# Eleven RMS norms of a two-block transformer: the row of factors by VectorE transposes and a broadcast through DRAM in place of PE products

## The chip, the cores and the metric

One core of a Trainium2 chip. The metric is the device time of one execution in microseconds (us). The engines are PE (matrix products; PEld is its weight load), VectorE (DVE), ScalarE (ACT), GpSimd (POOL) and SyncE (SP); each takes its instructions in the order in which the program has them, and they wait for one another by semaphores.

## What is computed

Two transformer blocks on 512 tokens of width 1024, in fp32. The first mixes by causal softmax attention of eight heads and by four recurrent heads (HGRN), then has a cross attention to a memory and a feed-forward layer; the second mixes by a convolution branch and a state-space branch (SSD, 8 groups of 256 channels) and has a gated feed-forward layer. The change touches two kinds of norm: that of each of the four recurrent heads over its 128 channels, and that of each of the eight groups of the state-space branch over its 256 channels.

```python
def rmsnorm(x, g):
    xf = x.astype(jnp.float32)
    y = xf * lax.rsqrt(jnp.mean(xf * xf, axis=-1, keepdims=True) + EPS)
    return (y * g.astype(jnp.float32)).astype(x.dtype)
...
        rec = hgrn2_chunkwise(gq, gf, gi, lbs[l])
        rec = rmsnorm(rec, hgrn_norm_g[l]) * jax.nn.silu(
            gg.astype(jnp.float32).reshape(b_, s_, HGRN_HEADS, HGRN_VAL_DIM))
...
    y = y * jax.nn.silu(z.astype(f32))
    yg = y.reshape(bsz, seqlen, N_GROUPS, D_INNER // N_GROUPS)
    yg = yg * lax.rsqrt(jnp.mean(yg * yg, axis=-1, keepdims=True) + RMS_EPS)
    y = (yg.reshape(bsz, seqlen, D_INNER) * norm_g.astype(f32)).astype(z.dtype)
    return y @ out_w
```

## The kernel before

Everything lies feature-major: a tile has 128 channels on its partitions and the 512 tokens along its free axis. A gemm (`gemm_tile`) makes one output tile of 128x512 from eight or more weight tiles of 128x128. To keep fp32 precision, weights and activations are split into a high and a low part, and each 128x128 tile is three products (`mm3`, L129 to L131; `wh`, `wl` are the halves of the weights, `xh`, `xl` those of the activations, which after the first block are also called `yh`, `yl` and `uh`, `ul`). A weight block of 128x1024 comes by a DMA on SP's queue, ACT makes its high half (L117), VectorE its low half (L118); each kind has three buffers. L180 and L181 split an activation in the same way.

A norm has four steps. `sq_acc` (L187) squares on ACT and adds up in `sqa` (128x512). `col_sum` (L196) adds over the 128 partitions on PE, four fp32 products with a 128x128 block of `sqa` as the weights and a column of ones (L202), so that the sums of the 512 tokens come out as 128x4. `rsqrt_col` (L206) scales them and adds epsilon on VectorE (`rv`, L208) and raises them to -1/2 on POOL (`rc`, L210). `row_bc` (L213) makes a row for all partitions of these columns, four fp32 products of 128x128 with the identity (L217), into the one PSUM buffer `pc`. A multiplication on VectorE reads it there (L479 in the recurrent heads, L911 in the groups). PE runs an fp32 product in two passes, and the trace has a record for each, so four products stand there as x8.

The first block runs the four recurrent heads (`hgrn_out`) and the attention (`fox`) as a background that is woven into the gemms. Of an attention pair, the scores are L498, the row maxima and sums on VectorE L508 to L516, the transposing products L519, the products with the values L531. Norms 0 and 1 fall near 147 to 170 us, norms 2 and 3 near 261 to 275 us.

The second block's state-space branch takes its 8 groups one after another (`group_a` to `group_b`), some 64 us each, woven into gemms as well. The norm of a group (`group_b`, L899) is done inside the next group's work. There VectorE makes `cb` (L849, the masked C by B product times `tri`), the chunk states `st` (L859 multiplies by the decay, L862 adds a product from PSUM; twice, for chunks 1 and 2 of 3) and the masked decays `mt` (L876); PE then makes the outputs of the group's two halves by products `mt,xd` and `Ct,st` (L885). POOL's queue brings the rows `ab` (L870) and `ep` (L891) from DRAM; ACT makes `mt` of `ab` (L874, L875).

The order of each engine's instructions is fixed when the program is built, by a scheduler that takes whatever is ready by priority; `tc.high_priority(-n)` lets a part come later. `HPRI` is 80, `APRI` 60, `BPRI` 120.

Of the kernel before, what the change touches and what calls it, by code (L numbers as in the profile page):

```python
# [64 lines left out]
def _build(tc, nc, es, a, out):  # L65
# [25 lines left out]
    def ctile(shape, dt, name):  # L91
        return const.tile(shape, dt, tag=name, name=name)

    vec = ctile([P, NVEC], F32, "vec")
    nc.scalar.dma_start(out=vec[:, 0:8], in_=a["vec"][:, 0:8])
    ones = ctile([P, P], F32, "ones")
    V.memset(ones, 1.0)
    mhalf = ctile([P, 4], F32, "mhalf")
    V.memset(mhalf, -0.5)
# [1 line left out]
    A.copy(out=warm, in_=ones[:, 0:4])  # L101
    ident = ctile([P, P], F32, "ident")
    nc.gpsimd.dma_start(out=ident, in_=a["ident"])
    tri = ctile([P, P], F32, "tri")
    nc.gpsimd.dma_start(out=tri, in_=a["tri"])

    def vcol(name, i=0, n=1):
        c, k = VEC[name]
        assert i + n <= k
        return vec[:, c + i:c + i + n]  # L110
# [76 lines left out]
    def sq_acc(accum, k, src, scale=1.0):  # L187
        if k == 0:
            A.activation(out=accum, in_=src, func=AF.Square, scale=scale)
        else:  # L190
            sq = nrm.tile([P, S], F32, tag="sq", name="sq")
            n = accum.shape[-1]
            A.activation(out=sq[:, :n], in_=src, func=AF.Square, scale=scale)
            V.tensor_tensor(out=accum, in0=accum, in1=sq[:, :n], op=ALU.add)
# [18 lines left out]
    def row_bc(col, nt, ms=mA):  # L213

        ps = ms()
        for j in range(nt):
            T.matmul(out=ps[:, j * P:(j + 1) * P], lhsT=col[:, j:j + 1].to_broadcast([P, P]), rhs=ident, start=True,  # L217
                     stop=True)
        return ps[:, :nt * P]

    def norm(srcs, n, nt, gain=None, eps=EPS, pl=None, rtag="R", ms=mA, late=0):

# [78 lines left out]
    with ExitStack() as ea:  # L301
# [163 lines left out]
        def hgrn_out(i, AT):  # L465
            ps = mA()
            for j in range(4):
                T.matmul(out=ps[:, j * P:], lhsT=iT[:, j, i * P:(i + 1) * P],  # L468
                         rhs=AT[:, ab(j, j):ab(j, j) + 4 - j, :].rearrange("p a b -> p (a b)"),
                         start=j == 0, stop=j == 3)  # L470
            o_ = hslot(4 + i)
            mix[4 + i] = o_
            A.copy(out=o_, in_=ps)
            ac = nrm.tile([P, S], F32, tag="sqa", name="sqa")
            sq_acc(ac, 0, o_)
            with tc.high_priority(-HPRI):
                r = rsqrt_col(col_sum(ac, 4, mC), 4, P)
            with tc.high_priority(-2 * HPRI):
                V.scalar_tensor_tensor(out=o_, in0=o_, scalar=vcol("hgrn_norm_g"), in1=row_bc(r, 4, mC), op0=ALU.mult,  # L479
                                       op1=ALU.mult)  # L480

        def fox(pairs):
            PT, nF = {}, {}
# [415 lines left out]
    def group_b(g, ys, zs):  # L899

        ac = nrm.tile([P, S], F32, tag="sqa", name="sqa")
        for e in range(2):
            V.tensor_tensor(out=zs[e], in0=ys[e], in1=zs[e], op=ALU.mult)
            sq_acc(ac, e, zs[e])
        with tc.high_priority(-APRI):
            r = rsqrt_col(col_sum(ac, 4, mC), 4, 256)
        with tc.high_priority(-BPRI):
            Rg = row_bc(r, 4, mC)
            res = []
            for e in range(2):  # L910
                V.scalar_tensor_tensor(out=zs[e], in0=zs[e], scalar=vcol("ssm_norm_g_2", 2 * g + e), in1=Rg, op0=ALU.mult,  # L911
                                       op1=ALU.mult)
                res.append(split_act(zs[e]))
        return res
# [214 lines left out]
def _pack(inp):  # L1129
    import numpy as np  # L1130

    def fm(w):
        K, N = w.shape
        return np.ascontiguousarray(w.reshape(K // P, P, N // P, P).transpose(2, 1, 0, 3))

    def tm(w):
        K, N = w.shape
        return np.ascontiguousarray(w.reshape(K // 256, 2, P, N // S, S).transpose(3, 0, 2, 1, 4))

    g = {}  # L1140
    i = {k: np.asarray(v) for k, v in inp.items()}
    g["xT"] = np.ascontiguousarray(i["x"][0].T)
    g["memT"] = np.ascontiguousarray(i["mem"][0].T)
    w = i["w_in"][0]
    o = [0, 512, 1024, 1536, 1544, 2056, 2568, 3080, 3592]
    p = [w[:, o[k]:o[k + 1]] for k in range(8)]
    g["w_fq"], g["w_fk"], g["w_fv"] = fm(p[0]), fm(p[1]), tm(p[2])[0]
    g["w_ff"] = np.pad(p[3].reshape(8, P, 8).transpose(1, 0, 2), ((0, 0), (0, 0), (0, 24)))
    g["w_gq"], g["w_gf"], g["w_gi"], g["w_gg"] = fm(p[4]), fm(p[5]), tm(p[6])[0], fm(p[7])
    wo = i["w_out"][0]  # L1150
    g["w_out"] = fm(np.concatenate([wo[512:], wo[:512]]))
    g["w_xq"], g["w_xo"], g["w1"], g["w2"] = fm(i["w_xq"][0]), fm(i["w_xo"][0]), fm(i["w1"][0]), fm(i["w2"][0])
    w = i["w_in_2"][0]
    g["w_glu"], g["w_z"], g["w_xs"] = fm(w[:, 0:2048]), fm(w[:, 2048:4096]), fm(w[:, 4096:6144])
    g["w_B"], g["w_C"], g["w_gate"] = fm(w[:, 6144:7168]), fm(w[:, 7168:8192]), fm(w[:, 8224:])
    g["w_dt"] = np.ascontiguousarray(w[:, 8192:8224].reshape(8, P, 32).transpose(1, 0, 2))
    g["w_pw"], g["w_so"], g["w_out2"] = fm(i["conv_pw_w_2"][0]), fm(i["ssm_out_w_2"][0]), fm(i["w_out_2"][0])
    g["w_gu"], g["w_dn"] = fm(i["w_gate_up_2"][0]), fm(i["w_down_2"][0])
    g["w_xk"], g["w_xv"] = fm(i["w_xkv"][0][:, :D]), tm(i["w_xkv"][0][:, D:])

    vec = np.zeros((P, NVEC), np.float32)

    def put(name, arr):
        c, k = VEC[name]
        vec[:arr.shape[0], c:c + k] = arr

    for name, k in _VEC_SHAPES:
        v = i[name]
        if name == "conv_dw_w_2":
            put(name, v[0].reshape(31, 8, P).transpose(2, 1, 0).reshape(P, 8 * 31))  # L1170
        elif name == "ssm_conv_w_2":
            put(name, v[0].reshape(4, 32, P).transpose(2, 1, 0).reshape(P, 32 * 4))
        elif name == "d_skip_2":
            put(name, np.repeat(v[0], 64).reshape(16, P).T)
        elif name in ("fox_f_bias", "dt_bias_2", "a_log_2"):
            put(name, v[0].reshape(-1, 1))
        else:
            put(name, v.reshape(-1).reshape(k, P).T)
    g["vec"] = vec

    r = np.arange(P)
    g["ident"] = np.eye(P, dtype=np.float32)
    g["tri"] = (r[:, None] <= r[None, :]).astype(np.float32)
    g["cmask"] = np.where(r[None, :] <= r[:, None], 0.0, NEG).astype(np.float32)
    lm = np.zeros((P, 7, 64), np.int32)
    for lv in range(7):
        n = 1 << lv
        t = r.reshape(-1, 2, n)[:, 1, :].reshape(-1)
        lm[:, lv, :] = (r[:, None] // (2 * n) == t[None, :] // (2 * n)) & (r[:, None] // n % 2 == 0)
    g["lmask"] = lm  # L1190
    return g
# [17 lines left out]
```

## Time and profile before

| | |
|---|---|
| median of 3 runs | 1927.7 us (1922.73 to 1928.18) |
| profiled execution | 1922.36 us, its span 1920.2 us |
| mean granted PE clock | 0.996 of full speed |
| busy share of the span | PE 99%, PEld 82%, DVE 63%, ACT 45%, POOL 5% |
| DMA | 208.84 MB, mean 109 GB/s |

The span runs from the first instruction to the last; all rows count from its start. Busy times of PE include the pipeline's fill, so records of products overlap, and what a product takes from PE is read from the start of one record to the start of the next. An entry in brackets at the end of a row of the timeline is the time for which the engine sat idle before it, and what ended that.

### The profile page before, as it was taken

Reading aid. Unit: us, or ns where it says so; the run is one execution under the profiler, and the core shown is the slowest. Engines: PE = TensorE matmul, PEld = TensorE weight load, DVE = VectorE, ACT = ScalarE, POOL = GpSimd, SP = SyncE. Lnnn points to the kernel's source line nnn. Section 1 sums busy time; section 2 is a strip of 40 time slices with the busy share of each in tenths; the row PEclk is TensorE's granted clock in tenths of the full one; section 3 lists DMA queues with packets and bytes.
Section 4 is the critical chain, followed back from the end, with each engine's and each line's share of the span. In section 5 each row is a group of like instructions: output and inputs, shape, how many; then the busy total and the mean of one; then the engine's idle time right before and its main releaser. Section 6 shows DMA issues by size and latency. Waiting matters only on the chain.

```text
span 1920.2 us, 25017 instructions
## 1 busy us (share of the span) xinstructions
PE 1894.2 (99%) x9640; PEld 1573.5 (82%) x9640; DVE 1208.8 (63%) x1886; ACT 860.0 (45%) x1395; POOL 98.2 (5%) x200
## 2 busy tenths in 40 slices
PE   8999999999999999999999999999999999999997
PEld 7787776877888888877888888888888988888897
DVE  6743756666442344468888989579997674424456
ACT  6523536444341233348545653445444652223344
POOL 1001110000000000011100110100000000000000
PEclk9999999999999999999999999999999999999999
DMA  7412211412223333334333333333245522233244
GB/s 254 137 56 79 75 45 47 140 55 77 94 93 99 99 99 103 113 98 139 121 111 115 113 118 104 107 108 109 98 138 184 163 98 99 83 115 95 92 130 146
DMA packets 67926, 208.84 MB, mean 109 GB/s; under 512 B 8536, under 2 KB 15960, under 8 KB 67808
## 3 DMA queue, kind: packets, MB, share of 16 engines
q1 hardware_dynamic: 58400, 184.61, 30.2%
q0 software_dynamic: 5808, 16.34, 2.7%
q10 hardware_dynamic: 3600, 6.30, 1.0%
q8 instruction: 76, 1.25, 0.3%
q14 instruction: 42, 0.34, 0.1%
HBM read 198.71 MB, written 8.54 MB: 108 GB/s over the span
## 4 chain that ended last, share of the span: by engine, by line
PE 91%; issue 3%; DVE 3%; ACT 1%; POOL 1%; DMA 1%; SPq 0%; POOLq 0%; DVEq 0%; ACTq 0%
PE acc L129 27%; PE acc L130 27%; PE acc L131 27%; PE pb L885 1%; PE pa L446 1%; PE pb L498 1%; PE pc L217 1%; DVE wl L118 1%; PE pa L855 1%; POOL rc L210 1%; PE pc L202 1%; PE pb L519 1%; PE pb L531 0%; PE pa L217 0%; PE pa L468 0%
## 5 line engine op out<-in xcount | busy, mean ns | idle before, releaser
L117 ACT CAST wh<-wr 128x1024 fp32r<-128x1024 f32 (+1 forms) x343 | 347.0, 1012 | 710.6 <-PE acc L130 584.6
L118 DVE TENSOR_TENSOR wl<-wr,wh 128x1024 fp32r<-128x1024 f32 (+1 forms) x343 | 403.7, 1178 | 279.0 <-ACT wh L117 275.4
L129 PE MATMUL acc<-yh,wh 128*128 128x512 f32 (+1 forms) x1112 | 433.4, 390 | 0.1
L131 PE MATMUL acc<-yh,wl 128*128 128x512 f32 (+1 forms) x1112 | 431.7, 388 | 0.0
L130 PE MATMUL acc<-yl,wh 128*128 128x512 f32 (+1 forms) x1112 | 430.2, 387 | 0.0
L130 PE MATMUL acc<-xl,wh 128*128 128x512 f32 (+1 forms) x832 | 313.7, 377 | 2.9 <-DVE xl L181 2.9
L129 PE MATMUL acc<-xh,wh 128*128 128x512 f32 (+1 forms) x832 | 314.9, 379 | 0.2 <-ACT xh L180 0.2
L131 PE MATMUL acc<-xh,wl 128*128 128x512 f32 (+1 forms) x832 | 314.6, 379 | 0.0
L129 PEld LDWEIGHTS acc<-yh,wh 128*128 128x128 f32 x1112 | 209.2, 188 | 41.8 <-issue 1.4
L131 PEld LDWEIGHTS acc<-yh,wl 128*128 128x128 f32 x1112 | 209.2, 188 | 40.7
L130 PEld LDWEIGHTS acc<-yl,wh 128*128 128x128 f32 x1112 | 209.2, 188 | 40.4 <-DVE yl L181 0.4
L129 PE MATMUL acc<-uh,wh 128*128 128x512 f32 (+1 forms) x520 | 184.1, 354 | 0.0
L131 PE MATMUL acc<-uh,wl 128*128 128x512 f32 (+1 forms) x520 | 183.9, 354 | 0.0
L130 PE MATMUL acc<-ul,wh 128*128 128x512 f32 (+1 forms) x520 | 183.9, 354 | 0.0
L130 PEld LDWEIGHTS acc<-xl,wh 128*128 128x128 f32 x832 | 157.6, 189 | 31.0 <-DVE xl L181 3.2
L776 DVE SCALAR_TENSOR_TENSOR cv<-gp,vec,cv 128x512 f32<-128x512 f32 x240 | 178.0, 749 | 6.0 <-ACT cv L774 3.0
L129 PEld LDWEIGHTS acc<-xh,wh 128*128 128x128 f32 x832 | 157.4, 189 | 29.4 <-issue 2.5
L131 PEld LDWEIGHTS acc<-xh,wl 128*128 128x128 f32 x832 | 157.5, 189 | 29.0 <-issue 2.7
L129 PEld LDWEIGHTS acc<-uh,wh 128*128 128x128 f32 x520 | 98.4, 189 | 13.5
L131 PEld LDWEIGHTS acc<-uh,wl 128*128 128x128 f32 x520 | 98.4, 189 | 13.5
L130 PEld LDWEIGHTS acc<-ul,wh 128*128 128x128 f32 x520 | 98.4, 189 | 13.3
L210 POOL TENSOR_TENSOR rc<-rv,mhalf 128x4 f32<-128x4 f32 (+1 forms) x25 | 27.8, 1114 | 972.2 <-DVE rv L208 888.0
(359 smaller groups left out, 2106.9 us busy)
## 6 DMA issues: line engine op xcount, KB each, us to landing
wr<-w SPq DMA_DIRECT2D x64, 512.0 KB, 3.8
wr<-w_gu SPq DMA_DIRECT2D x44, 512.0 KB, 3.4
wr<-w_out SPq DMA_DIRECT2D x24, 512.0 KB, 3.5
wr<-w_dn SPq DMA_DIRECT2D x24, 512.0 KB, 3.6
wr<-w_xs SPq DMA_DIRECT2D x16, 512.0 KB, 3.4
wr<-w_glu SPq DMA_DIRECT2D x16, 512.0 KB, 3.5
ab<-acsd POOLq DMA_DIRECT2D x32, 256.0 KB, 3.6
wr<-w_z SPq DMA_DIRECT2D x16, 512.0 KB, 3.5
```

Of the source, the lines that this page charges most:

```text
L117: A.copy(out=hi[:, :n], in_=raw[:, :n])
L118: V.tensor_tensor(out=lo[:, :n], in0=raw[:, :n], in1=hi[:, :n].bitcast(F32), op=ALU.subtract)
L129: T.matmul(out=ps, lhsT=lh, rhs=rh, start=start, stop=False)
L130: T.matmul(out=ps, lhsT=lh, rhs=rl, start=False, stop=False)
L131: T.matmul(out=ps, lhsT=ll, rhs=rh, start=False, stop=stop)
L202: T.matmul(out=ps[:, j:j + 1], lhsT=ac[:, j * P:(j + 1) * P], rhs=ones[:, 0:1], start=i == 0, stop=i == len(accs) - 1)
L210: G.tensor_tensor(out=r[:, :nt], in0=v[:, :nt], in1=mhalf[:, :nt], op=ALU.pow)
L217: T.matmul(out=ps[:, j * P:(j + 1) * P], lhsT=col[:, j:j + 1].to_broadcast([P, P]), rhs=ident, start=True, stop=True)
L446: T.matmul(out=ps[:, j * 64:(j + 1) * 64], lhsT=k_[:, j * P:(j + 1) * P], rhs=qv[:, j, :, 1, :], start=True, stop=True)
L498: T.matmul(out=ps[:, :n], lhsT=fq[p][es_, sl], rhs=fk[p][es_, 0:n], start=True, stop=True)
L519: T.transpose(out=pt[:, i * P:(i + 1) * P], in_=Sx[:, i * P:(i + 1) * P], identity=ident)
L776: yield V.scalar_tensor_tensor(out=o, in0=gp[:, t:t + S], scalar=cw(t), in1=o, op0=ALU.mult, op1=ALU.add)
```

## The change

A new function `rsqrt_far` replaces `col_sum`, `rsqrt_col` and `row_bc` in the four norms of `hgrn_out` and in `group_b` for the groups 0 to 6. VectorE transposes `sqa` in blocks of 32x32 (`tr`, L230), and adds up 32 neighbours, which gives 128x16 (L232). One fp32 product with the 0/1 matrix `mod32` (L234) adds the four partitions of equal number modulo 32 and gives the sums of 512 tokens as 32x16. VectorE scales (L236), POOL raises to -1/2 (L237), VectorE transposes the 32x32 block (L239), and 16x32 factors are written to DRAM by ACT's queue (2 KB, L241) and read back onto all 128 partitions by POOL's queue (256 KB, L242), into `Rh` or `Rg`. These two take buffers of the tag of `sqa`, `tr` one of the tag of `sq`; both tags have two. Group 7's norm stays as it was.

The multiplication by the factors has a later priority (-3 `HPRI` for -2 `HPRI`, -2 `BPRI` for -`BPRI`). `ones` becomes 128x4, `tri` bf16; `mod32` is loaded at the start (64 KB).

```diff
-    ones = ctile([P, P], F32, "ones")
+    ones = ctile([P, 4], F32, "ones")
...
-    tri = ctile([P, P], F32, "tri")
+    tri = ctile([P, P], BF16, "tri")
     nc.gpsimd.dma_start(out=tri, in_=a["tri"])
+
+    mod32 = ctile([P, P], F32, "mod32")
+    nc.gpsimd.dma_start(out=mod32, in_=a["mod32"])
+    r32 = ctile([32, 32], F32, "r32")
+    V.memset(r32, 0.0)
...
+    def rsqrt_far(ac, n, dst, eps=EPS, ms=mA):
+
+
+        tr = nrm.tile([P, S], F32, tag="sq", name="tr")
+        V.transpose(out=tr, in_=ac)
+        pt = nrm.tile([P, 16], F32, tag="p16", name="p16", bufs=1)
+        V.tensor_reduce(out=pt, in_=tr.rearrange("p (c i) -> p c i", i=32), axis=AX.X, op=ALU.add)
+        ps = ms()
+        T.matmul(out=ps[:, 0:16], lhsT=mod32, rhs=pt, start=True, stop=True)
+        v = tr[0:32, 32:48]
+        V.tensor_scalar(out=v, in0=ps[0:32, 0:16], scalar1=1.0 / n, scalar2=eps, op0=ALU.mult, op1=ALU.add)
+        G.tensor_tensor(out=r32[:, 0:16], in0=v, in1=mhalf[0:32, 0:1].to_broadcast([32, 16]), op=ALU.pow)
+        w = tr[0:32, 0:32]
+        V.transpose(out=w, in_=r32)
+        d = dram.tile([16, 32], F32, tag="rd", name="rd", bufs=4)
+        nc.scalar.dma_start(out=d, in_=w[0:16])
+        G.dma_start(out=dst, in_=d.rearrange("a b -> (a b)").unsqueeze(0).partition_broadcast(P))
...
+            R = nrm.tile([P, S], F32, tag="sqa", name="Rh")
             with tc.high_priority(-HPRI):
-                r = rsqrt_col(col_sum(ac, 4, mC), 4, P)
-            with tc.high_priority(-2 * HPRI):
-                V.scalar_tensor_tensor(out=o_, in0=o_, scalar=vcol("hgrn_norm_g"), in1=row_bc(r, 4, mC), op0=ALU.mult,
-                                       op1=ALU.mult)
+                rsqrt_far(ac, P, R, ms=mC)
+            with tc.high_priority(-3 * HPRI):
+                V.scalar_tensor_tensor(out=o_, in0=o_, scalar=vcol("hgrn_norm_g"), in1=R, op0=ALU.mult, op1=ALU.mult)
...
-        with tc.high_priority(-APRI):
-            r = rsqrt_col(col_sum(ac, 4, mC), 4, 256)
-        with tc.high_priority(-BPRI):
-            Rg = row_bc(r, 4, mC)
+        if g < 7:
+            Rg = nrm.tile([P, S], F32, tag="sqa", name="Rg")
+            with tc.high_priority(-APRI):
+                rsqrt_far(ac, 256, Rg, ms=mC)
+        else:
+            with tc.high_priority(-APRI):
+                r = rsqrt_col(col_sum(ac, 4, mC), 4, 256)
+        with tc.high_priority(-(2 * BPRI if g < 7 else BPRI)):
+            if g == 7:
+                Rg = row_bc(r, 4, mC)
```

Lines behind the new function are 23 higher in the changed kernel (L862 is L885 there, L885 is L908, L519 is L542).

Three places of the order. On VectorE, inside the second group's work, from `cb` to the first output of the group (`pc` holds the sums of the norm of the group before, `pa` products of this group). Before:

```order
L849 TENSOR_TENSOR cb<-pa,tri 128x512
L208 TENSOR_SCALAR rv<-pc 128x4
L876 TENSOR_TENSOR mt<-mt,cb 128x512
L859 TENSOR_TENSOR st<-st,cdb 128x256
L876 TENSOR_TENSOR mt<-mt,cb 128x512
L862 TENSOR_TENSOR st<-st,pa 128x256
L859 TENSOR_TENSOR st<-st,cdb 128x256
L862 TENSOR_TENSOR st<-st,pa 128x256
```

And now, at the same place:

```order
L872 TENSOR_TENSOR cb<-pa,tri 128x512
L236 TENSOR_SCALAR tr<-pc 32x16
L899 TENSOR_TENSOR mt<-mt,cb 128x512
L882 TENSOR_TENSOR st<-st,cdb 128x256
L899 TENSOR_TENSOR mt<-mt,cb 128x512
L885 TENSOR_TENSOR st<-st,pa 128x256
L239 STREAM_TRANSPOSE tr<-r_104 32x32
L882 TENSOR_TENSOR st<-st,cdb 128x256
L885 TENSOR_TENSOR st<-st,pa 128x256
```

The short transpose of the factors, which reads what POOL's power writes (`r_104`), now stands between the first and the second state update; in the norm of group 5 it stands directly behind `cb`.

On POOL at the same time, from the power of that norm on (`rd` is the row in DRAM). Before:

```order
L210 TENSOR_TENSOR rc<-rv,mhalf 128x4
L870 DMA ab<-acsd 128x512
L891 DMA ep<-eacd 64x384 x2
L870 DMA ab<-acsd 128x512 x2
```

And now:

```order
L237 TENSOR_TENSOR r_104<-tr,mhalf 32x16
L242 DMA Rg<-rd 128x512
L914 DMA ep<-eacd 64x384 x2
L893 DMA ab<-acsd 128x512 x2
```

The broadcast of the factors, which waits for the row in DRAM, stands ahead of the loads of `ep` and `ab`.

On PE, the end of the second attention half in the first block (`Sx` are the scaled weights, `PT` their transposes). Before:

```order
L519 MATMUL pb<-ident,Sx 128x128 x4
L131 MATMUL acc<-xh,wl 128x512
L129 MATMUL acc<-xh,wh 128x512
L519 MATMUL pb<-ident,Sx 128x128 x4
L531 MATMUL pb<-PT,vT 64x512 x2
```

And now:

```order
L136 MATMUL acc<-xh,wl 128x512
L542 MATMUL pb<-ident,Sx 128x128 x8
L521 MATMUL pb<-fk,fq 128x512 x2
L542 MATMUL pb<-ident,Sx 128x128 x8
L554 MATMUL pb<-PT,vT 64x512 x2
```

Before, gemm products stood between the two sets of transposing products of the last pair and ahead of the first; now none stands between the scores (L521) and the products with the values (L554).

## Rows read from the trace of the kernel before

**Rows 1.** The page, part 1: busy us, share of the span, instructions, by engine.
```profile
PE 1894.2 (99%) x9640; PEld 1573.5 (82%) x9640; DVE 1208.8 (63%) x1886; ACT 860.0 (45%) x1395; POOL 98.2 (5%) x200
```
**Rows 2.** The page, part 4: the chain that ended last, share by line.
```profile
PE acc L129 27%; PE acc L130 27%; PE acc L131 27%; PE pb L885 1%; PE pa L446 1%; PE pb L498 1%; PE pc L217 1%; DVE wl L118 1%; PE pa L855 1%; POOL rc L210 1%; PE pc L202 1%; PE pb L519 1%; PE pb L531 0%; PE pa L217 0%; PE pa L468 0%
```
**Rows 3.** A group's window: length, busy of PE, PEld, DVE, ACT, POOL, clock, DMA.
```profile
929.00:993.00 64.00, 64.00 (x343) 53.22 (x342) 56.22 (x81) 34.85 (x58) 6.33 (x14) 1.00 0.35 116
```
**Rows 4.** PE's timeline, norm 2: start, us, operation, [idle before <-releaser].
```profile
261.57 0.95 PE L202 MATMUL pc<-ones,sqa 128*128 128x1 f32 x8
262.38 0.49 PE L130 MATMUL acc<-xl,wh 128*128 128x512 f32 x1
...
266.21 1.16 PE L217 MATMUL pc<-ident,rc 128*128 128x128 f32 x8
267.12 0.47 PE L129 MATMUL acc<-xh,wh 128*128 128x512 f32 x1
```
**Rows 5.** PE's timeline, norm 1.
```profile
165.49 0.40 PE L129 MATMUL acc<-wh,xh 128*128 128x512 f32 x1
165.73 0.40 PE L130 MATMUL acc<-wl,xh 128*128 128x512 f32 x1
...
168.32 1.16 PE L217 MATMUL pc<-ident,rc 128*128 128x128 f32 x8 [0.84 <-POOL rc L210]
...
169.55 0.40 PE L131 MATMUL acc<-wh,xl 128*128 128x512 f32 x1
```
**Rows 6.** PE's timeline, norm 3.
```profile
271.95 0.49 PE L217 MATMUL pc<-ident,rc 128*128 128x128 f32 x2 [0.62 <-POOL rc L210]
272.36 0.49 PE L498 MATMUL pb<-fk,fq 64*128 64x128 f32 x4
272.79 1.57 PE L217 MATMUL pc<-ident,rc 128*128 128x128 f32 x6
274.01 0.78 PE L131 MATMUL acc<-xh,wl 128*128 128x512 f32 x1
```
**Rows 7.** Line L210: all its powers, shortest/median/longest in ns, and the forms.
```profile
L210 POOL TENSOR_TENSOR rc<-rv,mhalf x25: 695/1017/1987, 36.0 to 1909.7; 128x4 f32<-128x4 f32 x18, 128x2 f32<-128x2 f32 x7
```
**Rows 8.** Groups by line and form: busy us, mean ns of one, idle before.
```profile
L194 DVE TENSOR_TENSOR sqa<-sqa,sq 128x512 f32<-128x512 f32 x50 | 33.8, 688 | 2.6 <-ACT sq L193 1.7
```
**Rows 9.** PE's timeline, second group, first half's state products.
```profile
936.90 0.82 PE L885 MATMUL pb<-Ct,st 128*64 128x128 f32 x12
```
**Rows 10.** VectorE's timeline, second group.
```profile
933.24 0.69 DVE L849 TENSOR_TENSOR cb<-pa,tri 128x512 f32<-128x512 f32 x1 [0.66 <-PE pa L847]
...
934.58 0.42 DVE L859 TENSOR_TENSOR st<-st,cdb 128x256 f32<-128x256 f32 x1
...
936.49 0.42 DVE L862 TENSOR_TENSOR st<-st,pa 128x256 f32<-128x256 f32 x1
```
**Rows 11.** POOL's timeline, second group, the power of the norm before.
```profile
934.09 1.47 POOL L210 TENSOR_TENSOR rc<-rv,mhalf 128x4 f32<-128x4 f32 x1 [2.19 <-DVE rv L208]
```
**Rows 12.** Line L885: what its engine sat idle for (us, times).
```profile
  DVE st L862: 2.6, 7
```
**Rows 13.** DMA issues: line, KB of one, us from issue to landing (median).
```profile
ab<-acsd POOLq DMA_DIRECT2D x32, 256.0 KB, 3.6
...
gated<-gt ACTq DMA_DIRECT2D x16, 256.0 KB, 2.0
```
**Rows 14.** PE's timeline, first block, the longest stop of this stretch.
```profile
306.54 0.50 PE L130 MATMUL acc<-xl,wh 128*128 128x512 f32 x1 [2.94 <-DVE xl L181]
```
**Rows 15.** PE's timeline, the end of the second attention half.
```profile
320.42 0.50 PE L131 MATMUL acc<-xh,wl 128*128 128x512 f32 x1
...
324.64 0.60 PE L519 MATMUL pb<-ident,Sx 128*128 128x128 f32 x4
```
**Rows 16.** Windows behind the stop at 306.54, columns as in rows 3.
```profile
306.00:308.00 2.00, 1.46 (x4) 1.15 (x5) 2.00 (x6) 2.00 (x7) 0.00 (x0) 0.76 0.47 190
308.00:310.00 2.00, 2.00 (x7) 1.49 (x6) 2.00 (x6) 0.24 (x1) 0.00 (x0) 0.50 0.00 0
```

More of the change, by code (lines that the diff above doesn't have):

```diff
@@ L1183, in _pack @@
     g["tri"] = (r[:, None] <= r[None, :]).astype(np.float32)
+    g["mod32"] = (r[:, None] % 32 == r[None, :] % 32).astype(np.float32)
     g["cmask"] = np.where(r[None, :] <= r[:, None], 0.0, NEG).astype(np.float32)
```

## The prediction

> **What bounds the kernel now.** I read the page first. PE is busy for 1894.2 of 1920.2 us [rows 1], and in the chain that ended last the three products of the gemms have 27% each; small shares belong to norms: row products (L217) 1%, sums (L202) 1%, the power on POOL (L210) 1% [rows 2]. So every microsecond of PE that goes is a microsecond of the kernel, unless PE then stands still. Next come the windows by stage. In one of the eight groups (929 to 993 us) PE is busy for 64.00 of 64.00 us, but VectorE (DVE) for 56.22 [rows 3]: the engine to which the work moves has 7.8 us free there, not nearly half as the page's 63% suggests. Last I read PE's timeline around single norms, start to start, since a busy time there includes the pipeline.
>
> The profiled execution took 1922.36 us, 5.3 below the median of the runs, 1927.7. My sum is against 1922.36, and 5.3 is added at the end. A difference under 0.3% (5.8 us) is "same" here.
>
> **PE work removed.** Norm 2 of the recurrent heads is undisturbed. Its sums hold PE from 261.57 to 262.38, its row products from 266.21 to 267.12 [rows 4]: 0.81 + 0.91 = 1.72 us. I take this for nine norms: norms 0 and 2 and the seven of the groups, whose products are the same: 15.5 us. Norm 1 also keeps PE waiting: from 165.73 to 169.55, 3.82 us pass in which four ordinary gemm products start, 0.24 each (165.49 to 165.73), and 0.84 of it is a stop for the power [rows 5]. It costs 3.82 - 0.96 = 2.86. Norm 3 stops PE for 0.62 before 271.95; from there to 274.01 everything but a score product (272.36 to 272.79) is its own [rows 6]: 0.62 + 2.06 - 0.43 = 2.25, with sums 3.06. Together 21.4 us.
>
> **PE work added.** Eleven products of 16 columns. None of this shape is in the trace; the nearest is one of four column products in the 0.81 of [rows 4], 0.20. Bounds: 0.20 and an ordinary product's 0.24. 11 x 0.20 = 2.2. **Net 19.2 us** off PE, if nothing else waits.
>
> **VectorE work added.** A transpose and a reduction of 128x512, two short instructions. The nearest row for the big ones is an addition of that size, 0.69 [rows 8]; with their overlap some 1.2 together, from 0.9 to 1.4 if either runs a quarter faster or slower. In the group both stand ahead of the decay product `cb` (L849), in front of which VectorE idled for 0.66 [rows 10]; PE is the 0.6 us of the removed sums earlier, so of the 1.2 most lies in idle time, and `cb` stays near its old 933.24. If that cover were gone the next wait would grow by up to 0.6.
>
> **The new wait in a group.** This is the term that decides. In the order of VectorE, the short transpose L239 (behind the power) now stands between the first state update and the second pair of multiplication and update (L859, L862 before; lines from there on are 23 higher in the changed kernel, so L882, L885). VectorE runs in order, so both stand behind the power. POOL's power has 4 columns now and 16 afterwards. Of the 25 powers in the trace 18 have four columns and 7 have two; the median lasts 1.02, the shortest 0.70 [rows 7]. I read these as an undisturbed one of four and of two: 0.16 per column. So 16 columns: 1.02 + 12 x 0.16 = 2.9. Bounds: 1.0, if more columns cost nothing as only 32 of 128 partitions are used, and 4.1, in proportion. I take 2.9, the line through the two shapes that are there.
>
> In the group before, the power ran from 934.09 for 1.47, 0.45 longer than undisturbed, beside VectorE's multiplications [rows 11], and the state multiplication of 128x256 that fell into it took 0.42, as one of this size after it did [rows 10]: POOL gave way, VectorE did not. The Trainium skill has a rule that would cost more ("SBUF — State Buffer", section "Who interferes with whom"): a VectorE instruction with two SBUF inputs contends with a GpSimd instruction that reads SBUF, by an exclusive lock on a shared port pair. By the trace VectorE keeps its times and I add 0.45 to the power; by the rule, with the power the first to get the lock, VectorE would stand until its end, which is the third rival below. Afterwards: VectorE's scale instruction now directly behind `cb` ends at about 933.5; the power from 933.6 to 936.9 (2.9 + 0.4); L239 to 937.1; the state pair, two instructions of 0.42 [rows 10], to 937.9. PE wants that state for the last third of the 12 products Ct,st that began at 936.90 in the trace and took 0.82 [rows 9], at about 937.4; with 0.6 us less in front of it, at 936.8. **It waits 1.1 us in each of 7 groups: 7.7.** That PE already waits for this state is shown: idle 2.6 us in 7 cases until L862 [rows 12]. So a group keeps 1.72 - 0.20 - 1.1 = 0.4 of its gain.
>
> Behind that: the broadcast by DRAM starts with the write on ACT's queue at 937.1. The nearest transfers are 2.0 us (ACT's `gt` writes) and 3.6 (`ab`, a broadcast of the same 256 KB) [rows 13]; with 0.9 for two issues the row lands at about 943.6, bounds 941 and 947. VectorE reads it only 17 rows behind L239, more than 6 us of work, so I cost it at nothing. On POOL, L242 waits for the write and holds back `ep` and `ab` by about 3 us; `ab` feeds ACT, which is busy for 34.85 of 64 [rows 3]. That cover I also take as enough; without it up to 1 us per group.
>
> **The recurrent heads.** Norm 1's single product waits for VectorE behind norm 0's L239: 0.3. Norm 2's row takes 261.6 + 1.2 + 0.5 + 2.9 + 0.2 + 2.3 + 0.6 + 3.6 = 272.9 to land, write and broadcast as above; norm 2's multiplication stands on VectorE ahead of norm 3's L239 and of the second softmax scaling, which PE needed at about 271.3, where it stopped for the old norm 3. Part of this lies behind other products: 1.8 us. That old stop is in the 21.4 already.
>
> **The end of the second attention half.** Before, gemm products stood between the two transposing sets of L519; now (L542) they stand together behind the scores. From the end of the scores (320.42) to the second set (324.64) 4.2 us pass [rows 15], of which the four products of the first set take 0.46 by [rows 4]. So PE now stops for about 3.8. In return the moved gemm products come after it, and the splits of the mix before them: the stop of 2.94 for `xl` at 306.54 [rows 14] goes. Net +0.8 us.
>
> New waits: 7.7 + 0.3 + 1.8 + 0.8 = 10.6. Load of `mod32`, the smaller `ones`, bf16 `tri`: nothing, under the first loads. **Gain 19.2 - 10.6 = 8.6; 1922.36 - 8.6 = 1913.8, and against the median 1919.1 us.**
>
> **Rivals.**
> *The power is short.* If it takes 1.0, L239 comes at about 935 and delays nothing, and norm 2's row lands in time. Gain 19.2 - 0.8 = 18.4, so 1909.3. For it: a quarter of the partitions. Against: the slope between the two shapes.
> *The power stretches.* If all of it is slowed as in the group, by 1.47/1.02, it takes 4.2 and ends at 937.8; the wait becomes 2.0 per group, 14.0, and norm 3's 3.0: 18.1 with the other 1.1, gain 1.1, **1926.6: no change.** For it: [rows 11]. Against: VectorE soon stands at L239 and disturbs nobody.
> *VectorE is held back by the power, and PE's clock falls: slower.* If the 2.9 us power held the multiplications L876 and L859 until its end, the first products of the group, not only the last, would come 2.5 late. Behind a stop of 2.94 the granted clock was 0.76 and then 0.50 in stretches of 2 us, the lower of its two levels, 1.2 of 2.4 GHz [rows 14, 16]: 2 x (0.24 + 0.50) = 1.5 us lost. 7 x (2.5 + 1.5) = 28.0, with 2.9 of the other waits 30.9: 11.7 over the 19.2, so **1939.4**. It decides from 2.3 us lost per group ((19.2 - 2.9)/7). For it: the longer an instruction on POOL, the more of VectorE's fall into it. Against: the 0.42 inside the old power [rows 10, 11]. The Trainium skill's rule above would do just this; by that 0.42 the trace does not agree.
> *It does not do what it says.* If row and column sums stayed, the time would stay; the order shows all L217 of the 11 norms gone.
>
> **How the numbers follow.** My forecast has 0.48, the short power 0.20, the stretched one 0.20, the held VectorE 0.12. The forecast's own range is 1912 to 1926 (a wait of 0.3 to 1.9 in each group moves it by 5.6 either way, the other waits by half of them). Faster: 0.20, 0.38 of the forecast, 0.02 of the stretched: 0.60. Same: 0.10 + 0.16 = 0.26. Slower: 0.12 + 0.02 = 0.14. The range reaches to the short power and over the stretched one and leaves most of the held case out: 1907 to 1930.
>
> **What would show it.** PE busy for 19 less, products of L234 in slots of about 0.2; POOL's power with 16 columns near 2.9 and VectorE idle at L239 on it; PE idle in the seven groups before products of Ct,st, some 1.1 each, until VectorE's state update; PE idle before L542 near 320. A power near 1.0 or over 4, or idle time before the mt,xd products of a group with the clock down, would make me wrong, and so would ACT waiting for `ab` with PE behind it.

## The result and the profile after

The change made the kernel **slower**: 1936.36 us (median of 5 runs, 1932.18 to 1937.71) against 1926.62 for the kernel before on the same chip (5 runs, 1922.73 to 1928.18). The ratio is 1.0055, 95% interval 1.0038 to 1.0072: 0.55% more, clear of the noise. Forecast were 1919.1 and a range to 1930. The profiled execution took 1932.18 us, its span is 1930.4, at a mean granted clock of 0.995; it is set against the profiled execution of before, 1922.36 with a span of 1920.2: 10.2 us more span.

The page of the kernel after: busy time by engine, and the chain that ended last by line.

```profile
PE 1886.8 (98%) x9486; PEld 1551.7 (80%) x9486; DVE 1220.2 (63%) x1920; ACT 864.8 (45%) x1399; POOL 127.7 (7%) x212
...
PE acc L134 26%; PE acc L136 26%; PE acc L135 26%; POOL r L237 2%; PE pa L469 1%; DVE wl L123 1%; PE pb L908 1%; PE pb L521 1%; ACT wh L122 1%; DMA h<-xT 1%; PE pb L542 1%; PE pb L554 1%; PE pa L491 0%; DMA wr<-w_xk 0%; PE pa L222 0%
```

Against [rows 1] PE lost 154 records (the removed products had 176, the new ones have 22), but only 7.4 us of busy time where the forecast had 19; and the power on POOL (L237) has 2% of the chain. The new instructions, groups by line and form (busy us, mean ns of one | idle before):

```profile
L237 POOL TENSOR_TENSOR r<-tr,mhalf 32x16 f32<-32x16 f32 x11 | 34.7, 3154 | 179.6 <-DVE tr L236 179.6
L230 DVE STREAM_TRANSPOSE tr<-sqa 128x512 f32<-128x512 f32 x11 | 7.8, 708 | 6.2 <-ACT sqa L194 6.2
L232 DVE TENSOR_REDUCE p<-tr 128x16 f32<-128x512 f32 x11 | 7.5, 682 | 0.2
```

Waits for the state in the kernel before, then what PE waited for in the kernel after (us in all, times, longest):

```profile
PEld pb L885 <- DVE st L862: 2.6, 7, 0.4
```
```profile
PE pb L908 <- DVE st L885: 6.9, 6, 1.2
...
PE pb L542 <- DVE Sx L539: 5.5, 3, 3.0
...
PE pb L908 <- DVE mt L899: 1.6, 1, 1.6
...
PE pc L234 <- DVE nm L538: 1.0, 1, 1.0
```

The first line is the 2.6 us in 7 cases of [rows 12]: it belongs to PEld, the weight load. PE itself stood nowhere in the groups of the kernel before, so its stops at the state are new.

The stops at the state and at `Sx` are where the prediction put them, and its sum had them. They do not explain a loss, so I cut both traces at the starts of the same gemm products (the 7824 products of L129 to L131 before, of L134 to L136 after; all but 66 of them stand at the same place in the order) and compared what lies between. Every kernel below is the one before or after with the edit told in its place.

| us between the same products | before | after | after, `p16` moved |
|---|---|---|---|
| start | 131.39 | 133.22 | 131.22 |
| recurrent heads and attention | 221.02 | 220.71 | 221.30 |
| other gemms of the first block | 506.54 | 508.49 | 506.59 |
| start of the first group | 36.76 | 38.00 | 42.28 |
| groups | 501.78 | 504.36 | 501.74 |
| behind the groups (two stretches) | 200.40 | 201.92 | 201.31 |
| feed-forward layer, second block | 217.60 | 219.73 | 217.60 |
| end | 84.01 | 83.16 | 83.55 |

The row of the second feed-forward layer is the surprise: 960 gemm products, no norm of the change among them. Windows from the first of these to the last (length; busy us of PE, PEld, DVE, ACT, POOL with counts; clock; DMA share; GB/s), of before and of after:

```profile
1602.94:1820.54 217.60, 217.60 (x961) 180.25 (x960) 86.64 (x102) 63.67 (x82) 0.00 (x0) 1.00 0.31 97
```
```profile
1611.77:1831.50 219.73, 219.73 (x961) 180.30 (x960) 86.65 (x102) 63.73 (x82) 0.00 (x0) 1.00 0.31 96
```

PE never idles, the clock is 1.00 in both, the other engines do the same work, and yet a product takes 219.73/960 = 0.2289 us in place of 0.2267, 1% more. By the last column, which experiment 4 explains, such slots make 1.9 us in the first block, 2.6 in the groups, 0.6 behind them and 2.1 in the second block, and 0.4 comes back at the end: 6.9 of the 10.2 us.

### The profile page after: what moved, and what is told of

It reads as the page before. It is cut to its first block, busy times and chain, and to the rows that moved or that the text cites. A ratio compares the mean times of both kernels' runs of the same rounds, so it can differ in the third digit from the quotient of the medians.

```text
span 1930.4 us, 24766 instructions
## 1 busy us (share of the span) xinstructions
PE 1886.8 (98%) x9486; PEld 1551.7 (80%) x9486; DVE 1220.2 (63%) x1920; ACT 864.8 (45%) x1399; POOL 127.7 (7%) x212
## 4 chain that ended last, share of the span: by engine, by line
PE 87%; DVE 5%; issue 3%; POOL 2%; ACT 2%; DMA 1%; SPq 0%; POOLq 0%; DVEq 0%; ACTq 0%
PE acc L134 26%; PE acc L136 26%; PE acc L135 26%; POOL r L237 2%; PE pa L469 1%; DVE wl L123 1%; PE pb L908 1%; PE pb L521 1%; ACT wh L122 1%; DMA h<-xT 1%; PE pb L542 1%; PE pb L554 1%; PE pa L491 0%; DMA wr<-w_xk 0%; PE pa L222 0%
## 5 line engine op out<-in xcount | busy, mean ns | idle before, releaser
L134 PE MATMUL acc<-yh,wh 128*128 128x512 f32 (+1 forms) x1112 | 436.3, 393 | 0.5 <-DVE so L958 0.4
L136 PE MATMUL acc<-yh,wl 128*128 128x512 f32 (+1 forms) x1112 | 432.6, 389 | 0.0
L136 PE MATMUL acc<-xh,wl 128*128 128x512 f32 (+1 forms) x832 | 313.8, 377 | 0.3 <-DVE wl L123 0.3
L134 PE MATMUL acc<-xh,wh 128*128 128x512 f32 (+1 forms) x832 | 313.8, 378 | 0.3 <-DVE h L586 0.3
L136 PEld LDWEIGHTS acc<-yh,wl 128*128 128x128 f32 x1112 | 208.8, 188 | 44.8 <-issue 0.2
L134 PEld LDWEIGHTS acc<-yh,wh 128*128 128x128 f32 x1112 | 209.0, 188 | 43.7 <-issue 2.2
L134 PE MATMUL acc<-uh,wh 128*128 128x512 f32 (+1 forms) x520 | 184.9, 356 | 0.0
L136 PE MATMUL acc<-uh,wl 128*128 128x512 f32 (+1 forms) x520 | 184.1, 354 | 0.0
L134 PEld LDWEIGHTS acc<-xh,wh 128*128 128x128 f32 x832 | 157.2, 189 | 29.3 <-issue 1.3
L136 PEld LDWEIGHTS acc<-xh,wl 128*128 128x128 f32 x832 | 157.2, 189 | 28.9 <-issue 2.0
L136 PEld LDWEIGHTS acc<-uh,wl 128*128 128x128 f32 x520 | 97.5, 188 | 15.3 <-DVE wl L123 0.2
L134 PEld LDWEIGHTS acc<-uh,wh 128*128 128x128 f32 x520 | 97.7, 188 | 12.9
L673 DVE SCALAR_TENSOR_TENSOR t<-acc,R 128x512 f32<-128x512 f32 x32 | 22.0, 692 | 79.6 <-PE acc L136 78.6
```

Of the source, the lines that this page charges most:

```text
L134: T.matmul(out=ps, lhsT=lh, rhs=rh, start=start, stop=False)
L136: T.matmul(out=ps, lhsT=ll, rhs=rh, start=False, stop=stop)
L673: V.scalar_tensor_tensor(out=t, in0=ps, scalar=0.0, in1=R, op0=ALU.max, op1=ALU.mult)
```

## The experiments

The first theories were: the changed constants move every later tile by some bytes and this costs (A); a product's slot (from its start to the next one's) differs by chance from execution to execution (B); the new norms bring the longer slots (C). Later the first became: what counts is the distance, on each partition, between the weights' buffers (`wh`, `wl`) and those of the activations that stream past them (D), against the place of the weights by itself or the changed constants (E). A ratio is that on record for the runs of before in the same series; it differs by up to 0.0008 from the quotient of the two medians.

**1. The place of everything, by 32 bytes.** The kernel before with a shorter `ones`.

```diff
-    ones = ctile([P, P], F32, "ones")
+    ones = ctile([P, P - 8], F32, "ones")
```


> The kernel before with one edit: `ones` is 128x120 instead of 128x128, so every tile behind it lies 32 bytes lower (weights at a multiple of 64 bytes instead of 32 over one, as in the changed kernel). Theory A (place in memory): the start-to-start slot of the gemm products rises from 0.2267 to about 0.2289 us in long stretches, as in the changed kernel, and the time by about 7 us, to some 1933. Rival B (the slot differs from execution to execution by chance): time within 0.2% of before, slots mixed. Rival C (the new norms bring it): time and slots as before.

Measured: 1925.04 against 1924.45 us, ratio 0.9999 (0.9985 to 1.0012); the 960 products take 217.60. Moving everything together costs nothing.

**2. The changed constants without the changed norms.** After, with all eleven norms as before. `mod32`, `r32` and `tri` stay, and an unused `p16` keeps weights and activations at the places that they have in after.

```diff
+    p16 = nrm.tile([P, 16], F32, tag="p16", name="p16", bufs=1)
+    V.memset(p16, 0.0)
...
-                rsqrt_far(ac, P, R, ms=mC)
+                r = rsqrt_col(col_sum(ac, 4, mC), 4, P)
...
-                rsqrt_far(ac, 256, Rg, ms=mC)
+            r = rsqrt_col(col_sum(ac, 4, mC), 4, 256)
```


> The changed kernel with all eleven norms as before, but its constants (`ones` 128x4, `tri` bf16, `mod32`, `r32`) and its places in memory kept. Theory A (place in memory): about 7 us over before, slots 0.2289 in long stretches. Rivals B and C: as before within 0.2%. If the load of `mod32` costs something at the start (PE stood 2.45 instead of 0.29 us for the memory norm at 37 us), 1.9 us of it show here too.

Measured: 1933.97 us, ratio 1.0042 (1.0027 to 1.0058), 219.74 for the 960 products. Most of the loss is there with no new norm in the program.

**3. After, with everything 32 bytes higher** (a tile `pad` of 32 bytes ahead of `ones`).


> The changed kernel with 32 bytes of padding ahead of `ones`, so that the gemm operands lie 32 bytes over a multiple of 64 again. Theory A: slots back to 0.2267, about 7 us under the changed kernel, some 1929. Rivals B and C: as the changed kernel within 0.2%, 1936.

Measured: 1934.21 us, ratio 1.0047 (1.0031 to 1.0063), 219.74. The absolute place, by 32 bytes, does not matter here either.

**4. `p16` among the constants.** In the built program the weights `wh` begin at byte 49312 of a partition in the kernel before and at 49216 after, 96 lower, as the constants ahead of them shrank. The activations `uh` begin at 125344 and at 125312, only 32 lower: `p16`, 64 bytes, was added to the pool of the norms, which lies between. So the distance grew by 64 bytes, from 76032 to 76096. With `p16` ahead of the weights it is 76032 again, and every engine has the same instructions in the same order as in after:

```diff
+    p16 = ctile([P, 16], F32, "p16")
...
-        pt = nrm.tile([P, 16], F32, tag="p16", name="p16", bufs=1)
```


> The changed kernel with one edit: the 64-byte tile of the partial sums (`p16`) lies among the constants instead of behind `sqa` and `sq`. In the kernel before, the activations `uh`, `ul`, `yh`, `yl` lie 76032 bytes over the weights (a multiple of 128); in the changed kernel 76096 (64 more than a multiple of 128), here 76032 again; all weights still start at another place than before. Theory D (distance between the two operands, modulo 128 bytes): gemm slots back to 0.2267, 7 to 8 us under the changed kernel, about 1929. Rival E (absolute place of the weights, or `tri` in bf16, or `mod32`): as the changed kernel, 1936.

Measured: 1930.10 against 1926.13 us, ratio 1.0016 (1.0007 to 1.0026). The 960 products take 217.60. So the norms, with `p16` there, cost 3.1 us (1.3 to 5.0).

**5. The distance alone, in the kernel before.** 64 bytes less ahead of the weights, an unused tile of 64 bytes behind them: the activations stay in place.

```diff
-    ones = ctile([P, P], F32, "ones")
+    ones = ctile([P, P - 16], F32, "ones")
+    p16 = nrm.tile([P, 16], F32, tag="p16", name="p16", bufs=1)
+    V.memset(p16, 0.0)
```


> The kernel before with an unused 64-byte tile where the changed kernel has `p16`, and `ones` 64 bytes shorter to make room; nothing else. Distance of the activations from the weights 76096 bytes as in the changed kernel. Theory D: slots of 0.2289 in the same stretches as in the changed kernel, 7 to 8 us over before, about 1932. Rival E: as before.

Measured: 1931.30 against 1926.13 us, ratio 1.0026 (1.0016 to 1.0036), 5.0 us (3.1 to 6.9) for a tile that nothing uses.

**6. Distance or place of the weights?** In all slow kernels so far the weights lay 64 or 96 bytes lower as well. `before_both64` has only the shorter `ones` of experiment 5: weights and activations both 64 lower, the distance as before. `before_gap32`, `before_gap128`, `before_gap192` and `before_gap256` are experiment 5 with another number of bytes.

> The kernel before with ones 64 bytes shorter and no other tile: the weights wh, wl and the activations uh, ul, yh, yl both lie 64 bytes lower than before, their distance is that of before (594 x 128 bytes). If the distance decides, the 960 products of the second feed-forward layer take 217.60 us from first start to last, as before, and the profiled execution is at 1922 to 1926. If the place of the weights by itself decides (64 bytes lower, as in before_gap64 and after_pad32, where the slots were long), they take 219.73 and the execution 1927 to 1931.

> The kernel before with ones 32 bytes shorter and an unused tile of 32 bytes behind the weights: weights 32 bytes lower, activations in place, distance 32 more than a multiple of 128. If only distances of 64 more than a multiple of 128 are slow, the 960 products take 217.60; if every distance off a multiple of 64 or 128 is slow, 218.5 to 221. No sign known beforehand; the place of the weights alone has been tried 32 bytes lower (before_ones120, 217.60).

> The kernel before with ones 128 bytes shorter and an unused tile of 128 bytes behind the weights: weights 128 bytes lower, activations in place, distance 595 x 128 bytes. If the distance counts modulo 128, the 960 products take 217.60 as before; if a change of the distance by 64 or more as such is slow (a larger modulus), 219.7 or another time.

> As before_gap128, with 256 bytes in place of 128: weights 256 bytes lower, activations in place, distance 76288 bytes = 298 x 256. The 960 products of the second feed-forward layer took 217.60 us at a distance of 76032 = 297 x 256, 224.00 at 32 more, 219.74 at 64 more, 223.08 at 128 more. If the distance counts modulo 256, they take 217.60 again; if 76032 was good for another reason (a larger period, or the one distance itself), another time, 219 to 225.

> As before_gap128, with 192 bytes: distance 192 more than before. If the distance counts modulo 256 and both signs of it alike, the 960 products take what they take at 64 more (219.74); if they only grow with the distance to before, over 223.

| kernel | distance less 76032 | the 960 products, us | one product |
|---|---|---|---|
| before, both64 | 0 | 217.60, 217.60 | 0.2267 |
| gap32 | 32 | 224.00 | 0.2333 |
| gap64, after | 64 | 219.74, 219.73 | 0.2289 |
| gap128 | 128 | 223.08 | 0.2324 |
| gap192 | 192 | 224.00 | 0.2333 |
| gap256 | 256 | 217.60 | 0.2267 |

The distance decides, not the place of the weights: `before_both64` took 1921.59 us in its one execution, as before. The idea that multiples of 64 or 128 are good, on which experiments 5 and 6 were set up, fell: gap128 took 1944.03 and gap32 1945.16 us beside 1924.26 of before, gap192 1949.88 and gap256 1925.69 beside 1920.97, one execution each. 256 bytes more are as good as none (76032 is 297 x 256), and it is not symmetrical, since 192 is not 64. The kernel before stood on a good place. That the distance does it is also seen within one kernel. Two windows of gap32, one behind the other, of 240 products each; in the first the activations are `xh`, `xl`, which lie in front of the added tile and kept their distance to the weights, in the second `uh`, `ul`:

```profile
694.16:748.56 54.40, 54.40 (x241) 45.05 (x240) 25.69 (x30) 22.09 (x31) 0.00 (x0) 1.00 0.29 97
748.56:804.56 56.00, 56.00 (x241) 44.99 (x240) 22.60 (x26) 18.66 (x24) 2.23 (x4) 1.00 0.36 113
```

0.2267 and 0.2333 per product, from the same buffers of weights. The traffic of others is not what makes it. In after, during 122 of the 960 products no packet of a DMA was under way and VectorE, ScalarE and GpSimd stood still: their slots are 0.2290 in the mean, with 0.2289 for all; 110 such products of before have 0.2267. Why the distance between PE's own two operands counts stays open.

**7. The norms one kind at a time**, with `p16` among the constants: the heads' norms new and the groups' old, and the other way about.


> The changed kernel with `p16` among the constants and the groups' norms as before: only the four norms of the recurrent heads are new. In the profile of the run with `p16` moved, PE stands still for 9.3 us between 136 and 345 us instead of 4.8, and the stretch is as long as before. Theory: within 2 us of before. Rival (the forecast): 5.7 us under before. Rival (they hold the whole loss): 3 us over.

> The changed kernel with `p16` among the constants (gemm slots as before) and the four norms of the recurrent heads as before: only the seven norms of the groups are new. From the profile of the run with `p16` moved, the groups' stretch (901 to 1402 us) is as long as before: 1.14 us of stop each take the place of the products. Theory: within 2 us of before. Rival (the groups keep the 0.4 each of the forecast): 3 us under before. Rival (the groups hold the whole loss): 3 us over.

Measured: heads only 1926.29 us, ratio 1.0011 (0.9999 to 1.0024); groups only 1928.61 against 1925.65, ratio 1.0021 (1.0008 to 1.0033). Neither kind gains; the heads alone cannot be told from no change. With the groups' norms alone the groups take 501.42 us, no more than before; what this kernel loses lies at the start of the first group (41.21, see below).

**8. Two repeats**, to see what an execution changes by itself.


> The kernel before once more, for a second profile. Two stretches that no edit touches differ between the profiles so far: the memory norm near 37 us (PE stops 0.3 to 2.5 us and more, with half the clock behind it) and the start of the first group near 880 us (PE stops 0 to 4.2 us until ACT's `Bt`, behind the DMAs `cdd` and `ab`). If that is chance in when DMAs land, this profile may differ there from the first one of the same program; if it comes from the edits, it will not. Slots of 0.2267 in both cases.

> The changed kernel with `p16` among the constants once more, for a second profile: near 880 us the first had a stop of 4.15 us. If that is chance, it will be another length here.

Measured: 1924.38 and 1927.88 us. Of the stretches, the heads' took 221.02 in the first profile of before and 219.45 in the second: the first had one fall of the clock more (0.72, 0.50 and 0.92 in the windows from 272 to 278 us, 1.00 there in the second). The start of the first group took 36.76 and 38.67, as PE stopped 1.91 us for ACT's `Bt` in the second only. All other stretches agree within 0.3 but for the start (131.39 and 132.98), where the memory's norm near 37 us has its stops. The second profile with `p16` moved has 41.84 for the start of the first group, with a stop of 3.46 us where the first had 4.15.

**9. The power on 128 partitions.** The 512 sums as 128x4 in place of 32x16: four scale instructions write four blocks of partitions, the power is 128x4, four small DMAs write the row.

```diff
...
-        G.tensor_tensor(out=r32[:, 0:16], in0=v, in1=mhalf[0:32, 0:1].to_broadcast([32, 16]), op=ALU.pow)
...
+        for q in range(4):
+            V.tensor_scalar(out=v[32 * q:32 * q + 32], in0=ps[32 * q:32 * q + 32, 4 * q:4 * q + 4], scalar1=1.0 / n,
+                            scalar2=eps, op0=ALU.mult, op1=ALU.add)
+        G.tensor_tensor(out=r32[:, 0:4], in0=v, in1=mhalf, op=ALU.pow)
```


> The changed kernel with the power on 128x4 instead of 32x16 (each quarter of the partitions takes four of the sixteen columns: four short scale instructions, one transpose of 128x32, four small DMAs into the DRAM row). In the order the transpose then stands behind both state updates. Theory (the power stops VectorE ahead of the state): the power takes 1.0 to 1.5 us, the stop of PE of 1.14 us before the Ct,st products goes in six or seven groups, 7 to 8 us under the changed kernel, some 1928.5. Rival (PE would wait for something else there, or the slot of the gemms is all of it): under 3 us.

Measured: 1926.29 us, ratio 1.0011 (0.9997 to 1.0024), some 9 us under after at the same long slots. The heads' stretch falls from 220.71 to 215.46, the groups from 504.36 to 501.54. With `p16` among the constants as well:


> The power on 128x4 and `p16` among the constants, both edits. If they add up: 10 us (power) and 7 to 8 (place) under the changed kernel, about 1918.5, and 6 under before. If the place is not it, 1926.

Measured: 1919.91 us, ratio 0.9968 (0.9956 to 0.9981). The two edits add up.

**10. And the power earlier**: the kernel with both edits, and `tc.high_priority(60)` around the four scales and the power, which then stand ahead of other work on VectorE.


> As the run with both edits, and the four scale instructions and the power get a priority of +60 instead of -60, so that in a group they stand ahead of the four multiplications `xd`, `xw`, which cover the power. With the power on 128x4 alone the stop of PE had moved to the second half's mt,xd products (0.92 us in five groups, until VectorE's `mt`). Theory: that stop goes, 4 to 6 us less than with both edits, about 1913.5. Rival (PE then waits elsewhere, for `Rg` or `cb`): within 1.5 us of it.

Measured: 1915.85 against 1926.13 us, **ratio 0.9943 (0.9930 to 0.9956)**: faster than both kernels, by some 11 us under before. POOL's timeline of this kernel in the second group (start, us, operation, [idle before <-releaser]):

```profile
929.19 1.03 POOL L240 TENSOR_TENSOR r<-tr,mhalf 128x4 f32<-128x4 f32 x1 [3.91 <-DVE tr L238]
```

The power is over at 930.2, some 1 us before VectorE comes to its transpose (931.27), and the stop at the state is gone; the groups take 494.77 us, 7.0 less than before.

## Why the prediction was wrong

Forecast was a gain of 8.6 us, measured a loss of some 10. Two steps failed.

**One is the sentence "Load of `mod32`, the smaller `ones`, bf16 `tri`: nothing".** It priced the load and not the places, and it left out `p16`, the smallest tile of the change. By after against after with `p16` moved the place is worth 7.5 us (1.0055 less 1.0016, of 1926; a longer stop that came with the move, told below, works against this), by gap64 5.0 us (3.1 to 6.9), by the stretches 6.9: the largest part of the 10 us lost, and a term that the sum did not have. Nothing in the trace of before could give its size; that tiles move could be read from the diff.

**The other is the gain of 8.6 from the norms, which with `p16` moved cost 3.1 (1.3 to 5.0).** By size this is the larger error of the two, some 12 us. By the stretches it lies in the kept gain of the groups (2.9 forecast, 0 to 0.4 kept), in the heads (5.7 forecast, 1.9 lost) and in the start of the first group, which the prediction did not price.

*The group: the wait came out right, in part by luck.* The power was put at 2.9 undisturbed and 3.3 in the group. All eleven, shortest, median and longest in ns:

```profile
L237 POOL TENSOR_TENSOR r<-tr,mhalf x11: 2922/3292/3360, 150.0 to 1349.7; 32x16 f32<-32x16 f32 x11
```

So a power is paid by its columns, not by its elements: 128x4 and 32x16 have as many elements, and last 1.02 [rows 7] and 2.92. VectorE, POOL and PE in the second group of after, where [rows 9 to 11] have the kernel before:

```profile
937.61 0.69 DVE L872 TENSOR_TENSOR cb<-pa,tri 128x512 f32<-128x512 f32 x1 [0.25 <-PE pa L870]
938.22 0.15 DVE L236 TENSOR_SCALAR tr<-pc 32x16 f32<-32x16 f32 x1
...
938.45 3.36 POOL L237 TENSOR_TENSOR r<-tr,mhalf 32x16 f32<-32x16 f32 x1 [1.55 <-DVE tr L236]
...
938.94 0.43 DVE L882 TENSOR_TENSOR st<-st,cdb 128x256 f32<-128x256 f32 x1
...
941.18 0.61 PE L908 MATMUL pb<-Ct,st 128*64 128x128 f32 x8
...
941.84 0.20 DVE L239 STREAM_TRANSPOSE tr<-r 32x32 f32<-32x32 f32 x1 [1.53 <-POOL r L237]
941.98 0.37 DVE L882 TENSOR_TENSOR st<-st,cdb 128x256 f32<-128x256 f32 x1
942.46 0.42 DVE L885 TENSOR_TENSOR st<-st,pa 128x256 f32<-128x256 f32 x1
...
942.93 0.44 PE L908 MATMUL pb<-Ct,st 128*64 128x128 f32 x4 [1.14 <-DVE st L885]
```

These are the links that were forecast: the scale directly behind `cb`, the power, the transpose that waits for it, the second state pair, and PE 1.14 us late against a forecast of 1.1. Two slips cancelled in it. The power was put at 933.6, 0.4 behind the start of `cb` [rows 10], but the scale stood directly behind `cb` in the kernel before too, and its power began 0.85 behind [rows 11]; here it is 0.84. And PE came to the last four products not 3.6 behind the start of `cb`, as forecast, but 4.0 (the first eight records start at 941.18, two every 0.11 us, so the ninth was due at 941.62). That PE "already waits for this state" was a misreading: the waits of [rows 12] are those of its weight load.

In six of the seven groups a state multiplication fell into the power, and took 0.43 each time, where those outside took 0.37 to 0.43; so VectorE was not held back. POOL gave way, 3.36 for 2.92. By these rows the trace does not agree with the Trainium skill's rule on the exclusive lock ("SBUF — State Buffer", section "Who interferes with whom"), the third rival.

*The group: the kept gain was too large.* Forecast were 0.4 in each of seven, 2.9 in all; with `p16` moved the groups took 501.74 and 501.42 against 501.78, so 0 to 0.4 in all. Summed over the groups from PE's timeline (start of one record to start of the next, idle time apart), the old products gave back 11.1 us, where seven times 1.72 make 12.0; the new ones take 1.2; the idle time is 8.8, not 7.7, as the norm of group 5 waits 1.6 at `mt`; and the products `Ct,st`, into which the stop now falls, take 1.3 longer. That leaves 11.1 - 1.2 - 8.8 - 1.3 = -0.2; other products give some tenths.

*The heads: the stops were about right, the clock behind them was priced at zero.* PE's timeline of after:

```profile
272.16 0.33 PE L542 MATMUL pb<-ident,Sx 128*128 128x128 f32 x1 [2.08 <-DVE Sx L539]
...
324.56 2.07 PE L542 MATMUL pb<-ident,Sx 128*128 128x128 f32 x8 [3.02 <-DVE Sx L539]
```

Forecast were 1.8 and 3.8. Windows of 2 us behind each of the two stops, of after (columns as in [rows 3]):

```profile
274.00:276.00 2.00, 2.00 (x6) 1.52 (x6) 0.84 (x3) 1.48 (x4) 1.03 (x2) 0.50 0.00 0
324.00:326.00 2.00, 1.32 (x7) 0.98 (x7) 1.07 (x3) 1.21 (x4) 0.00 (x0) 0.70 0.00 0
326.00:328.00 2.00, 2.00 (x7) 0.76 (x8) 0.00 (x0) 0.76 (x3) 0.00 (x0) 0.50 0.00 0
```

A clock of 0.50 is 1.2 GHz, the lower level. The prediction had read such a fall in [rows 16] and priced it in a rival, not in its own stops. The old stop at 306.54 [rows 14] went, as forecast, and its fall with it; but two stand in its place. With `p16` moved, against the second profile of before, the heads' stretch gives back 6.6 us of norm products and takes 0.8 of new ones, 4.6 of idle time and 3.7 in attention products (`fk,fq`, `ident,Sx`, `PT,vT`) that fall into the slow stretches; gemm products give 0.6. So +1.9, where the forecast was 5.7 less than the first profile. That profile had a fall of the clock near 274 that the second has not, which makes 1.6 of the gap.

*Outside both: a stop that was not priced.* At the start of the first group PE stops for ACT's `Bt`: 0 to 1.91 us in the eleven profiles with old group norms (0.7 in the mean), 1.04 to 4.15 in the eight with new ones (2.9). Of these eight the three with `p16` in the pool of the norms have 1.04 to 2.72 and no fall of the clock, the five with `p16` among the constants 2.85 to 4.15 with one behind it. PE's timeline and two windows of the first profile with `p16` moved:

```profile
884.05 0.90 PE L853 MATMUL pa<-ident,Bt 128*128 128x128 f32 x3 [4.15 <-ACT Bt L777]
```
```profile
884.00:886.00 2.00, 1.95 (x8) 1.89 (x9) 0.73 (x2) 1.88 (x5) 0.12 (x1) 0.50 0.49 135
886.00:888.00 2.00, 2.00 (x11) 1.63 (x10) 1.68 (x4) 1.98 (x3) 0.00 (x0) 0.77 0.31 127
```

These five take 41.2 to 42.3 us for this stretch, the eleven 36.7 to 38.7. That is some 4 us, the largest single part of what the norms cost with `p16` moved; in after itself (38.00) little of it shows. The first of the new group norms comes only behind this stretch; by what way they or the place of `p16` lengthen the stop was not settled. Behind the groups 0.7 us more of idle time comes with the new norms, not followed further.

*The rivals.* VectorE was not held back by the power; a long stop with a fall of the clock came true all the same, in the heads and at the start of the first group, not within the groups. A short power does not exist at 32x16, but at 128x4 it does: experiments 9 and 10 are the first rival brought about by an edit, 6 and 11 us under before with `p16` among the constants.

## What to carry to other kernels

Before a difference is explained by the edit, cut both profiles at the same untouched products and compare their slots: 1% on every gemm is 7 us that no wait shows. A small new tile can move weights and activations against each other; put it where both move together, or try a few distances (here 256 bytes more were as good as none). Spread a power on POOL over the partitions, so that it has few columns, and reckon with the half clock behind a stop of 2 to 3 us on PE: here it came behind stops of 2.08 and 3.02, and not behind one of 2.72 (experiment 9, start of the first group).

## What the runs showed of the hardware that was not expected

A gemm product of 128x512 at full clock took 0.2267, 0.2289, 0.2324 or 0.2333 us in the mean of 960 (single slots 0.225 to 0.232 in after, 0.228 to 0.241 in gap128), by the distance between its two operands' buffers: up to 2.9%, or 20 us and more of this kernel. Products of 256 columns near the end did not follow this: 0.1237 before, 0.1217 in gap64 and 0.1210 in gap32 (means of 480, start to start), but 0.1237 in the kernel of experiment 2, which has the distance of gap64, and 0.1227 with `p16` moved, at the distance of before. A 32x32 transpose on VectorE took 0.20 us, one of 128x512 0.71, about as much as an addition of that size [rows 8]; the row of 2 KB reached DRAM in 1.3 us and came back to 128 partitions in 3.5 (medians), so the way through DRAM was never late in the groups.
